# A hybrid decoder block on one Trainium2 core: the first norm's row factors applied to results, a transposed copy of the input, and rearranged sums and buffers around the feed-forward part

## The chip, the cores and the metric

The kernel runs on one core of one Trainium2 chip. The metric is the device time of one execution in microseconds (us); the predicted number is the median of runs of the changed kernel. One core has a matrix engine (PE, TensorE), a vector engine (DVE, VectorE), an activation engine (ACT, ScalarE), a general engine (POOL, GpSimd) and an engine that here only issues transfers (SP). Each has its own queue, worked off in order; transfers run on 16 DMA engines.

## The reference

```python
h = rms_norm(x, norm_mix_w)                 # x: 1024 rows x 1024
proj = h @ w_in                             # queries, K/V, gates, retention q/k/v/gate, merge gates
o_a = nsa_attention(...)                    # compressed, selected and window branches
y_a = o_a @ w_nsa_branch                    # 512 -> 1024
o_r = head_group_norm(retention(...)) * silu(g_ret)
y_b = o_r @ w_ret_branch                    # 1024 -> 1024
gate_a, gate_b = split(sigmoid(g_merge))
x = x + (gate_a * y_a + gate_b * y_b) @ w_mix_out
h = rms_norm(x, norm_ffn_w)
u = causal_dwconv(h @ w_ffn_up)             # 1024 -> 2 x 2816, width 3
x = x + (silu(u_gate) * u_val) @ w_ffn_down # 2816 -> 1024
return rms_norm(x, norm_final_w)
...
def rms_norm(x, w):
    return x * rsqrt(mean(x * x, -1) + EPS) * w
```

All values are float32. `rms_norm` is a row factor times x times a gain for each column, so a product of `h` with weights is the row factor times the product of (x times gain) with them.

## The kernel before

**Products.** A float32 value is held as two parts, a high one (rounded to fp32r by ACT) and a low one (the difference, from DVE or POOL): `split` (L174). Each product of 128 rows by 512 columns and 128 of depth is three matmuls, high by high, high by low, low by high (`mm3`, L278). Weights come by a 512 KB transfer into one of two raw slots (`wraw`), and are then split into five pairs of slots `wh`, `wl` (`Weights`, L181).

**Stages in the order of time.** (1) For each of eight row tiles x is loaded, squared and summed on ACT, brought to a row factor by small DVE steps (`normed`, L262), multiplied on DVE, transposed by eight PE transposes (`transposed_split`, L269) and split into `hh`, `hl`. (2) Projections of keys and values, block compression, queries. (3) Attention, by a planner that sets the order; the merge gates' raw projections (L784) fill PE between and go to DRAM as `gate_d`. (4) Retention. (5) The merges: first stage, eight steps (L1006 to L1018), each a gate loaded and passed through a sigmoid (`gated`, L976), 24 matmuls with `w_a` into one of two 1024-wide PSUM tiles (`ps2`), a DVE multiply that frees that tile (L1012), and eight transposes of `o_r` with their splits; second stage, eight steps of 48 matmuls with `w_b` (L1031 to L1042). (6) The output projection `w_mix` in two halves of columns (L1122, L1139), the second with the second norm and the transposes (`piece`, L1078). (7) The up projection for 22 column tiles f (`up`, L1235), and (8) the down projection in seven groups (`PRODUCTS`, L1408).

**Seven products in place of eight.** Up and down are each cut into 2 by 2 blocks and computed with seven products of sums of blocks. For down the sums of weight blocks (t1 to t4) are made ahead and put in DRAM: `t_sums` (L986), one for each j below 11: four loads of 256 KB, four DVE subtractions and four stores. For up the weights' sums are made just before use (`other_weights`, L1210), and those of activations in `sums` (L1154), after subtractions between row pieces in `piece`. The first product of each of five tiles (`LEAD`, L1191) runs before the sums are ready. Two lines of this make tiles wait for each other:

```python
m = mp.tile([P, S], F32, name=f"ma{j % KT}" if j < KT else "gb", bufs=1 if j < KT else 3)
...
(mp.tile([P, S], F32, name="tq", tag="gb", bufs=3) for _ in range(2))
```

The raw weight sums `tq` and the gates of the second stage share three slots `gb`; the first stage's gates have eight tiles `ma0` to `ma7` of their own. All transfers go through SP's queue in the order in which the scheduler puts them; one that waits for its slot holds up those behind it.

Of the kernel before, what the change touches and what calls it, by code (L numbers as in the profile page):

```python
# [14 lines left out]
OP = mybir.AluOpType  # L15
# [148 lines left out]
def hybrid_block(ctx: ExitStack, tc: tile.TileContext, a, c, out):  # L164
# [153 lines left out]

    with tc.tile_pool(name="n1", bufs=2, side="right") as n1:
        gain = n1.tile([P, D], F32, name="gain1", bufs=1)  # L320
        for t in range(NT):
            xt = big.tile([P, D], F32, name="big")
            n = 2 if t == 0 else 1
            for i in range(0, D, D // n):
                nc.sync.dma_start(xt[:, i:i + D // n], a["x"][0, t * P:(t + 1) * P, i:i + D // n])
            if t == 0:
                nc.sync.dma_start(gain, bcast_rows(a["norm_mix_w"][0], D))
                nc.sync.dma_start(ident, c["ident"])
            h = big.tile([P, D], F32, name="big")
            normed(n1, xt, gain, h, n)  # L330
            transposed_split(psA, h, hh, hl, t)
            if t < 2:
                kvw.more()
                kvw.more()
# [42 lines left out]
    def k_store(b, t, ps):  # L377

        ks = np_.tile([P, G, DH], F32, name="ks", bufs=2)
        nc.scalar.activation(ks, ps, AF.Copy)  # L380
# [12 lines left out]

    def v_store(b, t, ps):
        split(vhl[b][:, t, :, 0:DH], vhl[b][:, t, :, DH:], ps)
# [6 lines left out]
    def evac_kv(t, ps):  # L402
        nc.scalar.activation(kvc[:, t].rearrange("p a g d -> p (a g d)"), ps[:, 0:256], AF.Copy)
        k_store("s", t, g64(ps[:, 256:384]))
        v_store("s", t, g64(ps[:, 384:512]))
# [4 lines left out]
    def evac_kw(t, ps):  # L410
        k_store("w", t, g64(ps[:, 0:128]))
        v_store("w", t, g64(ps[:, 128:256]))
        nc.vector.tensor_copy(gates[:, t].rearrange("p h b -> p (h b)"), ps[:, 256:280])
# [90 lines left out]
    def evac_q(t, ps):  # L504
        nc.scalar.activation(qsb[:, t].rearrange("p h d -> p (h d)"), ps, AF.Copy, scale=DH ** -0.5)
        rope16(qsb[:, t], t, H, np_)
# [296 lines left out]
    nc.sync.dma_start(rope, c["rope128"])  # L803
    dmask = rp.tile([P, RH, P], F32, name="dmask")
# [26 lines left out]
    for p in range(2):  # L831
# [48 lines left out]
        def values(t, ps):  # L880
            v = big.tile([P, 2, 2, DV], F32R, name="v", tag="big")
            split(v[:, 0], v[:, 1], ps.rearrange("p (h e) -> p h e", h=2))
# [121 lines left out]
    for ch in range(2):  # L1004
        nx = Weights(w_a, 0, 4, [(512, 512)]) if ch == 0 else Weights(w_b, 0, KT, [(0, 512)])
        for i in range(4):  # L1006
# [7 lines left out]
            if len(t_left) > 5:  # L1014
                x, y = ([q[:, 0:512], q[:, 512:S]] for q in
                        (mp.tile([P, S], F32, name="tq", tag="gb", bufs=3) for _ in range(2)))
                t_sums(t_left.pop(0), x, y)
            transposed_split(ps1, o_r[ch * 4 + i], *orT, ch * 4 + i)  # L1018
        gw = nx
    with ort:  # L1020
# [8 lines left out]
        for ch in range(2):  # L1029
            nx = Weights(w_b, 0, KT, [(512, 512)]) if ch == 0 else Weights(w_mix, 0, KT, [(0, 512)])  # L1030
            for i in range(4):  # L1031
# [10 lines left out]
                ml.append(mlj)  # L1042
            gw = nx
# [34 lines left out]
    def piece(t, h):  # L1078
# [18 lines left out]
        side = nc.vector if t == NT - 1 else nc.gpsimd  # L1097
        nc.vector.tensor_tensor(b11, b12, b11, OP.subtract)
        side.tensor_tensor(b12, b22, b12, OP.subtract)
        nc.vector.tensor_tensor(b22, b22, b11, OP.subtract)  # L1100
        side.tensor_tensor(b21, b21, b22, OP.subtract)
# [65 lines left out]
    def raw_up(f, i):  # L1167
        r = wraw.tile([P, 2, 512], F32, name="wr")
        nc.sync.dma_start(r.rearrange("p a b -> p (a b)"), a["w_ffn_up"][f][:, i * 1024:(i + 1) * 1024])
        return r  # L1170

    def first_weights(f):

        g = raw_up(f, 0)
        p = parts2(g, nc.gpsimd)
        return {k: [x[:, i] for x in p] for i, k in enumerate(("a11", "a12"))}, g
# [12 lines left out]
    sums([4, 5])  # L1189
    uw, begun = {}, {}  # L1190
    for f in range(LEAD):  # L1191
        uw[f], _ = first_weights(f)
        begun[f] = start_up(uw[f])
# [9 lines left out]
    cpool = ups.enter_context(tc.tile_pool(name="cp", bufs=8, reuse_waits="tile"))  # L1203
# [6 lines left out]
    def other_weights(f, w, g=None):  # L1210
        v = raw_up(f, 1)
        g = g or raw_up(f, 0)
# [22 lines left out]
    def up(f, w, begun=None):  # L1235
        x, p1 = begun or start_up(w)
# [12 lines left out]
        if not begun:  # L1249
            prod(x, w["a12"], "21", False, True)  # L1250
# [12 lines left out]
    def weights(f):  # L1263
        if f in uw:
            return other_weights(f, uw.pop(f))
        return other_weights(f, *first_weights(f))

    nx = weights(0)
    for f in range(FT):
        w, nx = nx, weights(f + 1) if f + 1 < FT else None  # L1270
        up(f, w, begun.pop(f, None))
    tp.close()
    ups.close()


    STEPS = [(j, min(2, HT - j)) for j in range(0, HT, 2)]
    NS = len(STEPS)
# [5 lines left out]
    W = {"b11": (0, 0), "b21": (1, 0), "b22": (1, 1)}  # L1283
    A = {"a11": (0, 0), "a12": (1, 0), "a21": (0, 1), "a22": (1, 1)}
    kept = {}

    def fetch_a(k, i, dst):
# [3 lines left out]
        return dst  # L1291

# [33 lines left out]
    def prepared(sk, tk, i):  # L1326
        j, n = STEPS[i]
        t = wraw.tile([P, 2, 512], F32, name="wr")
        if tk in W:
            kh, nh = W[tk]  # L1330
            r0 = (kh * HT + j) * P
            src = w_dn[r0:r0 + n * P, nh * 512:nh * 512 + 512].rearrange("(k p) n -> p k n", p=P)
        else:
            src = t_d[int(tk[1]) - 1][j:j + n].rearrange("k p n -> p k n")
        nc.sync.dma_start(t[:, :n], src)
# [78 lines left out]
    ready = {}  # L1414
# [4 lines left out]
    for at, (i, j) in enumerate(units):  # L1419
# [3 lines left out]
        if i == 1:  # L1423
            held("a21", j)
# [40 lines left out]
_LAYOUT = {"w_ffn_up": _up_layout}  # L1465
# [22 lines left out]
```

## Time and profile before

| | |
|---|---|
| runs | 1814.02, 1811.32, 1814.24 us, median 1814.02 |
| the profiled execution | 1812.5 us, span 1810.7 us |
| PE busy | 1750.6 us (97%) |
| DVE, ACT, POOL busy | 1186.5, 804.2, 126.6 us |
| mean granted PE clock | 0.99 of full speed (2.4 GHz) |
| transfers | 178.88 MB |

The profile is of one execution. Its busy time of PE is time in which a matmul was in the engine, at whatever clock was granted; what PE did not do in the span is 60 us. Times in the rows below are from the span's start.

### The profile page before, as it was taken

The page shows a single profiled execution, that of the slowest core. Times are in us where ns is not written, and L with a number is a line of the kernel's source. Part 1 is how long each engine was busy: PE and PEld are TensorE (multiplying, and loading weights), DVE is VectorE, ACT ScalarE, POOL GpSimd, SP SyncE. Part 2 cuts the span into 40 slices and gives each one's busy share as a digit, 9 for nine tenths or more (in the row PEclk, how much of TensorE's full clock was granted, in tenths as well). Part 3 has the DMA queues.
Part 4 walks back from the last instruction along what each step waited for, and adds up shares of the span by engine and source line. Part 5 has one row for each costly group of instructions (what it writes and reads, how often), then busy time and mean ns, then how long its engine had stood idle before and what let it go on. Part 6 is the DMA issues. An engine that isn't in the chain of part 4 may idle for free.

```text
span 1810.7 us, 22500 instructions
## 1 busy us (share of the span) xinstructions
PE 1750.6 (97%) x8331; PEld 1434.6 (79%) x8331; DVE 1186.5 (66%) x2337; ACT 804.2 (44%) x1464; POOL 126.6 (7%) x78
## 2 busy tenths in 40 slices
PE   7999999999999999999989999789999999999998
PEld 6987888888788888888868877667888888878886
DVE  7445877777875554455644446767767777678666
ACT  6334666666662344136332215434444444343344
POOL 0000020110100000000000002301121211000000
PEclk9999999999999999999989999899999999999999
DMA  6121010110202111101682383322322322395353
GB/s 227 55 82 53 19 56 32 36 59 18 71 24 94 47 37 57 47 1 47 231 270 93 93 300 137 99 70 70 104 71 82 93 70 87 108 354 189 94 163 111
DMA packets 87418, 178.88 MB, mean 99 GB/s; under 512 B 8508, under 2 KB 18316, under 8 KB 87308
## 3 DMA queue, kind: packets, MB, share of 16 engines
q1 hardware_dynamic: 87308, 177.44, 30.2%
q8 instruction: 65, 1.06, 0.2%
q14 instruction: 45, 0.37, 0.1%
HBM read 137.57 MB, written 39.85 MB: 98 GB/s over the span
## 4 chain that ended last, share of the span: by engine, by line
PE 60%; DVE 5%; DMA 4%; ACT 2%; issue 2%; SPq 1%; POOL 1%; DVEq 0%; POOLq 0%; ACTq 0%
PE f L283 33%; PE mm L283 19%; PE fill L772 2%; DMA tq<-in_w_ffn_down 2%; PE po L826 1%; PE pv L718 1%; PE pt L706 1%; PE sc L610 1%; DMA wr<-in_w_ffn_up 1%; PE pst L826 1%; DMA wr<-in_w_mix_out 0%; ACT wh L209 0%; PE pss L871 0%; DVE c L1231 0%; DVE c L1232 0%
## 5 line engine op out<-in xcount | busy, mean ns | idle before, releaser
L283 PE MATMUL mm<-wh,hh 128*128 128x512 f32 (+1 forms) x576 | 224.0, 389 | 0.5 <-ACT hh L175 0.5
L283 PE MATMUL mm<-wh,hl 128*128 128x512 f32 (+1 forms) x576 | 219.8, 382 | 0.0
L283 PE MATMUL mm<-wl,hh 128*128 128x512 f32 (+1 forms) x576 | 219.8, 382 | 0.0
L209 ACT ACTIVATE wh<-wr 128x1024 fp32r<-128x1024 f32 (+1 forms) x72 | 74.6, 1037 | 167.0 <-PE mm L283 83.2
L713 DVE TENSOR_TENSOR pl<-pt,ph 128x512 fp32r<-128x512 f32 (+1 forms) x148 | 100.6, 686 | 41.8 <-ACT ph L710 41.2
L283 PEld LDWEIGHTS mm<-wh,hl 128*128 128x128 f32 x576 | 108.8, 189 | 20.6 <-DVE hl L176 0.3
L283 PEld LDWEIGHTS mm<-wh,hh 128*128 128x128 f32 x576 | 108.8, 189 | 20.2 <-ACT hh L175 0.9
L283 PE MATMUL f<-wh,sh 128*128 128x512 f32 x308 | 121.6, 395 | 3.3 <-ACT sh L175 3.3
L710 ACT ACTIVATE ph<-pt 128x512 fp32r<-128x512 f32 (+1 forms) x148 | 87.7, 594 | 82.8 <-PE pt L706 74.5
L283 PEld LDWEIGHTS mm<-wl,hh 128*128 128x128 f32 x576 | 108.9, 189 | 19.5 <-DVE wl L215 0.5
L283 PE MATMUL f<-wl,sh 128*128 128x512 f32 x308 | 121.5, 395 | 0.0
L283 PE MATMUL f<-wh,sl 128*128 128x512 f32 x308 | 120.7, 395 | 0.0
L283 PE MATMUL f<-bh,wh 128*128 128x512 f32 x264 | 105.0, 398 | 11.9 <-ACT c L1186 11.9
L176 POOL TENSOR_TENSOR wl<-wr,wh 128x1024 fp32r<-128x1024 f32 x22 | 53.6, 2438 | 898.3 <-ACT wh L175 883.4
L283 PE MATMUL f<-bht,wh 128*128 128x512 f32 x264 | 104.8, 397 | 8.3 <-ACT wh L175 8.3
L772 PE MATMUL fill<-hh,wh 128*128 128x512 f32 x256 | 104.5, 408 | 3.0 <-ACT sg L784 2.0
L283 PE MATMUL f<-bht,wl 128*128 128x512 f32 x264 | 105.0, 398 | 2.2 <-DVE wl L176 2.2
L628 ACT ACTIVATE big<-big,st 128x640 f32<-128x640 f32 (+7 forms) x128 | 93.4, 730 | 28.1 <-DVE st L624 27.3
L215 DVE TENSOR_TENSOR wl<-wr,wh 128x1024 fp32r<-128x1024 f32 (+1 forms) x60 | 71.5, 1193 | 51.2 <-ACT wh L209 50.2
L283 PE MATMUL f<-blt,wh 128*128 128x512 f32 x264 | 104.4, 395 | 0.0
L283 PE MATMUL f<-bl,wh 128*128 128x512 f32 x264 | 104.1, 394 | 0.0
L283 PE MATMUL f<-bh,wl 128*128 128x512 f32 x264 | 103.4, 393 | 0.0
(282 smaller groups left out, 4127.6 us busy)
## 6 DMA issues: line engine op xcount, KB each, us to landing
wr<-in_w_ffn_up SPq DMA_DIRECT2D x49, 512.0 KB, 4.7
wr<-in_w_in SPq DMA_DIRECT2D x40, 512.0 KB, 3.7
tq<-in_w_ffn_down SPq DMA_DIRECT2D x44, 256.0 KB, 4.7
t<-tq SPq DMA_DIRECT2D x44, 256.0 KB, 3.0
act<-c SPq DMA_DIRECT2D x22, 512.0 KB, 2.8
wr<-t SPq DMA_DIRECT2D x20, 512.0 KB, 3.5
a<-act SPq DMA_DIRECT2D x33, 256.0 KB, 6.0
gate<-sg SPq DMA_DIRECT2D x32, 256.0 KB, 2.0
```

Source lines behind the costliest of these rows:

```text
L176: (engine or nc.vector).tensor_tensor(lo, src, f32(hi), OP.subtract)
L209: nc.scalar.activation(hi[:, :, :self.n], self.raw[len(self.hi)], AF.Copy)
L215: self.engine.tensor_tensor(lo[:, :, :self.n], self.raw[j], f32(self.hi[j][:, :, :self.n]), OP.subtract)
L283: nc.tensor.matmul(ps, stat(sp, kt), mov(mp, kt), start=(first and n == 0), stop=(last and n == 3 * nk - 1), skip_group_check=more)
L610: nc.tensor.matmul(out[:, c0:c0 + n], q[:, h, :], mov, start=(q is box["h"]), stop=(q is box["l"]))
L628: nc.scalar.activation(probs[b][h], probs[b][h], AF.Exp, scale=-1.0, bias=stat["nm", b][:, h:h + 1], accum_out=stat["w", b][:, h:h + 1])
L706: nc.tensor.transpose(bx["pt"][:rows, h, :], probs[h][:, k * P:k * P + rows], ident)
L710: nc.scalar.activation(bx["h"][:rows], bx["pt"][:rows], AF.Copy)
L713: nc.vector.tensor_tensor(bx["l"][:rows], bx["pt"][:rows], f32(bx["h"][:rows]), OP.subtract)
L718: nc.tensor.matmul(acc["pv"], v, bx[part][:rows].rearrange("p h q -> p (h q)"), start=start, stop=stop)
L772: nc.tensor.matmul(fx["ps"], w.at(sp, kt, i * P, P), hT[mp][:, kt, half * 512:half * 512 + 512], start=(n == 0), stop=(n == 3 * KT - 1))
L826: nc.tensor.matmul(ps[:, h, :], stat[sp][:, h, :], mov[mp][:, h, :], start=(first and n == 0), stop=(last and n == 2))
```

## The change

**Row factors.** x is loaded twice: transposed (`x_t`, a second copy in DRAM that the host prepares) in pieces of 128 columns, that is rows of 512 bytes, and as before. The transposed tile times the gain (now one value for a partition) is split directly into `hh`, `hl`. The row factor `rs` is computed beside it and multiplied in where results leave PSUM: as the scale of ACT's copies, in `scaled_split`, in the two halves of retention's table `rope`, in the branch gates. For the merge gates, which lie transposed in DRAM, `rs` goes to DRAM and comes back broadcast (`rb`), and POOL multiplies each loaded gate by it before the sigmoid.

**Weight sums of down.** In the first merge stage every second step makes one (4, before the first 6), three are made in the second stage in `ma` tiles that are no longer needed, and four in the output projection at t = 0, 1, 2, 4 (before 5, at t = 1, 3, 5, 6, 7). The `gb` ring has two slots in place of three.

**Up and down.** All of `piece`'s subtractions are on DVE, `sums` stands behind the loop over the five first products; the second half of the weights, v, has its own two slots, the first half g is loaded a second time for every f (before: for f below 5) and its sums are made in place; the ring `c4` has 6 tiles in place of 8. Down's first pair of operands is fetched and split ahead of the last `up`.

```diff
+            xt = big.tile([P, KT, P], F32, name="big")
+            src = a["x_t"].rearrange("(k p) s -> p k s", p=P)[:, :, t * P:(t + 1) * P]
...
+                nc.sync.dma_start(xt[:, ks], src[:, ks])
+                if t == 0 and k == 0:
+                    kvw.fetch()
+                nc.vector.tensor_mul(xt[:, ks], xt[:, ks],
+                                     gain[:, ks, None].to_broadcast([P, KT // n, P]))
+                split(hh[:, ks, t * P:(t + 1) * P], hl[:, ks, t * P:(t + 1) * P], xt[:, ks])
...
-            normed(n1, xt, gain, h, n)
-            transposed_split(psA, h, hh, hl, t)
...
+            nc.sync.dma_start(x, a["x"][0, t * P:(t + 1) * P, :])
+            *_, v = mean_square(n1, [x], [x])
+            nc.vector.tensor_copy(rs[:, t:t + 1], rstd_of(n1, v))
...
+    def scaled_split(hi, lo, src, t):
+        r = rs[:, t:t + 1]
+        nc.scalar.activation(hi, src, AF.Copy, scale=r)
+        nc.vector.scalar_tensor_tensor(lo, src, r, f32(hi), op0=OP.mult, op1=OP.subtract)
...
+    for i in range(2):
+        nc.vector.tensor_mul(rope[:, i], rope[:, i], rs[:, :, None].to_broadcast([P, NT, DK // 2]))
...
-            nc.scalar.activation(sg, ps, AF.Silu)
+            nc.scalar.activation(sg, ps, AF.Silu, scale=rs[:, t:t + 1])
...
+    rb = mp.tile([P, S], F32, name="rb")
+    nc.sync.dma_start(rb, bcast_rows(rs_d, S))
...
-        m = mp.tile([P, S], F32, name=f"ma{j % KT}" if j < KT else "gb", bufs=1 if j < KT else 3)
+        m = mp.tile([P, S], F32, name=f"ma{j % KT}" if j < KT else "gb", bufs=1 if j < KT else 2)
         nc.sync.dma_start(m, gate_d[j])
+        nc.gpsimd.tensor_tensor(m, m, rb, OP.mult)
         nc.scalar.activation(m, m, AF.Sigmoid)
...
-            if len(t_left) > 5:
+            if (ch * 4 + i) % 2 == 0:
...
+                if j in (2, 4, 6):
+                    x, y = ([q[:, 0:512], q[:, 512:S]] for q in
+                            (mp.tile([P, S], F32, name="tq", tag=f"ma{j - k}") for k in (2, 1)))
+                    t_sums(t_left.pop(0), x, y)
...
-        if t in (1, 3, 5, 6, 7) and len(t_left):
+        if t in (0, 1, 2, 4):
...
-    sums([4, 5])
...
-            t = waiting[0][0]
             piece(*waiting.pop(0))
-            sums([t])
-        prod(begun[f][0], uw[f]["a12"], "21", False, True)
+        prod(begun[f][0], fw[f]["a12"], "21", False, True)
+    sums([4, 5, 6])
+    sums([7])
...
-    cpool = ups.enter_context(tc.tile_pool(name="cp", bufs=8, reuse_waits="tile"))
+    cpool = ups.enter_context(tc.tile_pool(name="cp", bufs=6, reuse_waits="tile"))
...
+        v = cpool.tile([P, 2, 512], F32, name="v", bufs=2)
+        nc.sync.dma_start(v.rearrange("p a b -> p (a b)"), a["w_ffn_up"][f][:, 1024:])
+        g = raw_up(f)
...
-        s2 = c4()
-        nc.vector.tensor_sub(s2[:, 0], g[:, 0], v[:, 0])
-        nc.vector.tensor_sub(s2[:, 1], g[:, 1], s[:, 1])
-        p = parts2(s2, nc.vector)
+        nc.vector.tensor_sub(g[:, 0], g[:, 0], v[:, 0])
+        nc.vector.tensor_sub(g[:, 1], g[:, 1], s[:, 1])
+        p = parts2(g, nc.vector)
...
+        if f == FT - 1:
+            s = fetch_a("a11", 0, wraw.tile([P, 2, 512], F32, name="wr"))
+            ready[0, 0] = [parts2(s, nc.vector), parts2(fetch_t("b11", 0), nc.vector)]
+        up(f, w)
```

How the order of instructions moves is shown at three places.

**SP's queue, start of the first merge stage.** `ma` are gates, `tq` the loads of a weight sum, `t` its stores, `rb` the broadcast row factors. Before:

```order
L978 DMA ma_8544<-gate_1643 128x1024
L989 DMA tq<-in_w_ffn_down 128x512
...
L978 DMA ma_8601<-gate_1644 128x1024
L997 DMA t_8523<-tq 128x512
L989 DMA tq<-in_w_ffn_down 128x512
L990 DMA tq<-in_w_ffn_down 128x512
L997 DMA t_8525<-tq 128x512
L997 DMA t_8524<-tq 128x512
L997 DMA t_8526<-tq 128x512
L978 DMA ma_8658<-gate_1645 128x1024
```

After:

```order
L1002 DMA rb<-rs_d 128x1024
L1006 DMA ma_8474<-gate_1569 128x1024
L1018 DMA tq<-in_w_ffn_down 128x512
...
L1006 DMA ma_8532<-gate_1570 128x1024
L1026 DMA t_8453<-tq 128x512
L1006 DMA ma_8576<-gate_1571 128x1024
L1026 DMA t_8455<-tq 128x512
L1026 DMA t_8454<-tq 128x512
L1026 DMA t_8456<-tq 128x512
L1006 DMA ma_8634<-gate_1572 128x1024
```

Before, all four stores and two of the next sum's loads stand ahead of the third gate; after, the third gate stands behind one store, and the next sum's loads behind the fourth gate.

**ACT's queue around the first evacuation of the five first products** (L1186 before, L1217 after, both `p1`; `bht` are high parts of `sums`, `h,ss` squares of the second norm, `rs_s` its square root, `wh` an up weight). Before:

```order
L256 ACTIVATE h,ss<-c_9866 128x512
L175 ACTIVATE bht_10398<-pc 128x4x128 x2
L256 ACTIVATE h,ss<-c_10324 128x512
L175 ACTIVATE bht_10400<-pc 128x4x128
L233 ACTIVATE rs_s<-rs_v 128x1
L175 ACTIVATE bht_10400<-pc 128x4x128
L175 ACTIVATE bht_10402<-pc 128x4x128 x2
L175 ACTIVATE bht_10404<-pc 128x4x128 x2
L1186 ACTIVATE c_10441<-f 128x512
```

After:

```order
L256 ACTIVATE h,ss<-c_9826 128x512
L175 ACTIVATE bht_10342<-pc 128x4x128
L175 ACTIVATE wh<-wr 128x1024
L256 ACTIVATE h,ss<-c_10268 128x512
L175 ACTIVATE bht_10342<-pc 128x4x128
L175 ACTIVATE bht_10344<-pc 128x4x128
L233 ACTIVATE rs_s<-rs_v 128x1
L1217 ACTIVATE c_10369<-f 128x512
```

Five `bht` fewer stand between the square root and this copy, three in place of eight ahead of it in all, and one weight's high part more.

**DVE's queue in the up stage** (a weight sum is L1214 to L1220 before, L1246 to L1251 after, with `wl`, its low part; L1240, L1244, L1248 before, L1271, L1275, L1279 after take products out of PSUM; L1259 and L1290 are the last multiply of the tile before). Before:

```order
L1215 TENSOR_TENSOR c_10802<-c_10802,wr 128x512
L1219 TENSOR_TENSOR c_10809<-wr 128x512
L1220 TENSOR_TENSOR c_10809<-wr,c_10802 128x512
L1259 TENSOR_TENSOR c_10787<-c_10787,c_10792 128x1024
L176 TENSOR_TENSOR wl<-c_10802,wh 128x1024
L176 TENSOR_TENSOR wl<-c_10809,wh 128x1024
L1240 TENSOR_TENSOR c_10833<-f,c_10502 128x512
```

After:

```order
L1247 TENSOR_TENSOR c_10744<-c_10744,wr 128x512
L1271 TENSOR_TENSOR c_10774<-f,c_10422 128x512
L1250 TENSOR_TENSOR wr<-wr,v 128x512
L1290 TENSOR_TENSOR c_10729<-c_10729,c_10734 128x1024
L176 TENSOR_TENSOR wl<-c_10744,wh 128x1024
L1251 TENSOR_TENSOR wr<-wr,c_10744 128x512
L1275 TENSOR_TENSOR c_10789<-f,c_10774 128x512
L1279 TENSOR_TENSOR c_10805<-f,c_10789 128x512
L176 TENSOR_TENSOR wl<-wr,wh 128x1024
```

Before, a whole weight sum with both low parts stands ahead of the next products' copies; after, copies stand between its steps.

## Rows read from the trace of the kernel before

**Rows 1.** Busy time by stretches: length, each engine's busy time, clock, DMA.

```profile
core 0: us, PE busy (x) PEld busy (x) DVE busy (x) ACT busy (x) POOL busy (x), PEclk, DMA share, GB/s
...
20.00:66.50 46.50, 46.50 (x236) 37.97 (x235) 27.56 (x94) 22.88 (x67) 1.48 (x4) 1.00 0.37 119
...
872.20:911.30 39.10, 39.10 (x194) 32.32 (x194) 25.58 (x33) 14.85 (x19) 0.00 (x0) 1.00 0.91 304
911.30:934.40 23.10, 15.30 (x57) 11.25 (x57) 15.61 (x21) 7.26 (x11) 0.00 (x0) 0.85 0.85 286
934.40:951.00 16.60, 16.57 (x51) 11.62 (x52) 3.87 (x5) 4.24 (x4) 0.00 (x0) 0.69 0.68 236
951.00:1027.60 76.60, 76.60 (x340) 63.42 (x339) 33.56 (x28) 20.89 (x20) 0.00 (x0) 1.00 0.24 75
...
1193.00:1238.00 45.00, 34.51 (x131) 25.88 (x131) 33.81 (x40) 16.43 (x19) 2.59 (x2) 0.93 0.32 105
1238.00:1584.80 346.80, 346.80 (x1502) 281.89 (x1502) 252.35 (x287) 148.09 (x161) 62.07 (x34) 1.00 0.27 85
```

**Rows 2.** Waits of PE over the span: total, times, longest.

```profile
PE f L283 <- ACT c L1186: 11.9, 4, 7.0
PE tp L275 <- DVE big L267: 8.7, 1, 8.7
PE f L283 <- ACT wh L175: 8.3, 4, 3.6
PE mm L283 <- DVE ma L1012: 4.8, 3, 2.6
PE f L283 <- ACT sh L175: 3.3, 1, 3.3
PE tp L275 <- DVE orT L176: 3.0, 2, 2.5
```

**Rows 3.** Timeline of PE and ACT in the first 22 us.

```profile
8.65 1.97 PE L275 MATMUL tp<-ident,big 128*128 128x128 f32 x8 [8.65 <-DVE big L267]
11.15 0.80 PE L283 MATMUL mm<-wh,hh 128*128 128x512 f32 x1 [0.54 <-ACT hh L175]
...
17.26 1.03 PE L275 MATMUL tp<-ident,big 128*128 128x128 f32 x8
18.19 0.50 PE L283 MATMUL mm<-wl,hh 128*128 128x512 f32 x1
...
15.81 1.06 ACT L209 ACTIVATE wh<-wr 128x1024 fp32r<-128x1024 f32 x1 [1.31 <-DMA wr<-in_w_in]
```

**Rows 4.** Chain that ended last, in the merges: start, us, what.

```profile
875.66 4.89 DMA tq<-in_w_ffn_down
...
917.53 6.05 DMA ma<-gate
923.60 1.07 ACT ma L979
```

**Rows 5.** Timeline of DVE and POOL around 1123 and 1134 us.

```profile
1123.66 2.19 DVE L239 SCALAR_TENSOR_TENSOR rs_t<-rs_y,rs_v 128x1 f32<-128x1 f32 x1
...
1134.32 0.21 DVE L239 SCALAR_TENSOR_TENSOR rs_t<-rs_y,rs_v 128x1 f32<-128x1 f32 x1
...
1123.42 2.42 POOL L176 TENSOR_TENSOR wl<-wr,wh 128x1024 fp32r<-128x1024 f32 x1 [1.02 <-ACT wh L175]
```

**Rows 6.** Groups of DVE's instructions from 872 to 951 us.

```profile
L993 DVE TENSOR_TENSOR tq<-tq 128x512 f32<-128x512 f32 x6 | 4.1, 686 | 2.3 <-DMA tq<-in_w_ffn_down 2.3
```

**Rows 7.** Timeline of ACT around the merge to the up stage.

```profile
1077.57 1.06 ACT L209 ACTIVATE wh<-wr 128x1024 fp32r<-128x1024 f32 x1 [9.70 <-DMA wr<-in_w_mix_out]
...
1133.07 2.69 ACT L175 ACTIVATE bht<-pc 128x512 fp32r<-128x512 f32 x5
1135.67 0.57 ACT L1186 ACTIVATE c<-f 128x512 f32<-128x512 f32 x1
```

More of the change, by code (lines that the diff above doesn't have):

```diff
@@ L379, in k_store @@
         ks = np_.tile([P, G, DH], F32, name="ks", bufs=2)
-        nc.scalar.activation(ks, ps, AF.Copy)
+        nc.scalar.activation(ks, ps, AF.Copy, scale=rs[:, t:t + 1])
         rope16(ks, t, G, np_)
@@ L394, in v_store @@
     def v_store(b, t, ps):
-        split(vhl[b][:, t, :, 0:DH], vhl[b][:, t, :, DH:], ps)
+        scaled_split(vhl[b][:, t, :, 0:DH], vhl[b][:, t, :, DH:], ps, t)
     kvc = np_.tile([P, NT, 2, G, DH], F32, name="kvc")
@@ L504, in evac_q @@
     def evac_q(t, ps):
-        nc.scalar.activation(qsb[:, t].rearrange("p h d -> p (h d)"), ps, AF.Copy, scale=DH ** -0.5)
+        nc.scalar.activation(qsb[:, t].rearrange("p h d -> p (h d)"), ps, AF.Copy,
+                             scale=rs_q[:, t:t + 1])
         rope16(qsb[:, t], t, H, np_)
@@ L1013, in hybrid_block @@
             ma.append(m)
-            if len(t_left) > 5:
+            if (ch * 4 + i) % 2 == 0:
                 x, y = ([q[:, 0:512], q[:, 512:S]] for q in
-                        (mp.tile([P, S], F32, name="tq", tag="gb", bufs=3) for _ in range(2)))
+                        (mp.tile([P, S], F32, name="tq", tag="gb", bufs=2) for _ in range(2)))
                 t_sums(t_left.pop(0), x, y)
@@ L1248, in up @@
         nc.vector.tensor_add(cv[:, 1], z, u3)
-        if not begun:
-            prod(x, w["a12"], "21", False, True)
+        if f >= LEAD:
+            prod(x, fw[f]["a12"], "21", False, True)
         nc.scalar.activation(cg[:, 0], x, AF.Copy)
@@ L1261, in up, with fetch_a, fetch_t @@
         nc.sync.dma_start(act_d[f], yg)
[L1263 to L1268, printed above, removed]
-    for f in range(FT):
-        w, nx = nx, weights(f + 1) if f + 1 < FT else None
-        up(f, w, begun.pop(f, None))
+    STEPS = [(j, min(2, HT - j)) for j in range(0, HT, 2)]
+    NS = len(STEPS)
+    A = {"a11": (0, 0), "a12": (1, 0), "a21": (0, 1), "a22": (1, 1)}
+    W = {"b11": (0, 0), "b21": (1, 0), "b22": (1, 1)}
+    def fetch_a(k, i, dst):
+        (kh, sh), (j, n) = A[k], STEPS[i]
+        for x in range(n):
+            nc.sync.dma_start(dst[:, x], act_d[kh * HT + j + x][:, sh])
+        return dst
+    def fetch_t(k, i):
+        j, n = STEPS[i]
+        t = wraw.tile([P, 2, 512], F32, name="wr")
+        if k in W:
+            kh, nh = W[k]
+            r0 = (kh * HT + j) * P
+            src = w_dn[r0:r0 + n * P, nh * 512:nh * 512 + 512].rearrange("(k p) n -> p k n", p=P)
+        else:
+            src = t_d[int(k[1]) - 1][j:j + n].rearrange("k p n -> p k n")
+        nc.sync.dma_start(t[:, :n], src)
+        return t
+    ready = {}
+    nx = other_weights(0)
+    for f in range(FT):
+        w, nx = nx, None
+        if f + 1 < FT:
+            if f + 1 >= LEAD:
+                fw[f + 1] = first_weights(f + 1)
+            nx = other_weights(f + 1)
+        if f == FT - 1:
+            s = fetch_a("a11", 0, wraw.tile([P, 2, 512], F32, name="wr"))
+            ready[0, 0] = [parts2(s, nc.vector), parts2(fetch_t("b11", 0), nc.vector)]
+        up(f, w)
     tp.close()
     ups.close()
-    STEPS = [(j, min(2, HT - j)) for j in range(0, HT, 2)]
-    NS = len(STEPS)
     keep = ctx.enter_context(tc.tile_pool(name="keep", bufs=1, side="right", reuse_waits="tile"))
@@ L1282, in hybrid_block @@
     kp2 = ctx.enter_context(tc.tile_pool(name="keep2", bufs=1, reuse_waits="tile"))
-    W = {"b11": (0, 0), "b21": (1, 0), "b22": (1, 1)}
-    A = {"a11": (0, 0), "a12": (1, 0), "a21": (0, 1), "a22": (1, 1)}
     kept = {}
-    def fetch_a(k, i, dst):
-        (kh, sh), (j, n) = A[k], STEPS[i]
-        for x in range(n):
-            nc.sync.dma_start(dst[:, x], act_d[kh * HT + j + x][:, sh])
-        return dst
     def held(k, i):
@@ L1326, in prepared @@
     def prepared(sk, tk, i):
[L1327 to L1335, printed above, removed]
+        n = STEPS[i][1]
+        t = fetch_t(tk, i)
         s = S_OF[sk](i)
@@ L1423, in hybrid_block @@
         if i == 1:
+            held("a11", j)
             held("a21", j)
@@ L1481 @@
     a = {k: given(k, _LAYOUT.get(k, lambda v: v)(v)) for k, v in inputs.items()}
+    a["x_t"] = given("x_t", inputs["x"][0].T)
     c = {k: given("c_" + k, v) for k, v in _constants().items()}
```

63 lines of the change are left out of this document (33 added, 30 removed).

## Prediction

> **What bounds the kernel now.** I read the busy time by stretches first. PE is the bound nearly everywhere: from 1238 to 1584.8 us it is busy for all of 346.8 us while DVE works 252.35, ACT 148.09 and POOL 62.07 [rows 1]. There only fewer or faster matmuls help, and attention and retention read the same way. What can be gained lies in the few stretches in which PE has less to do than the stretch is long, and in those at a low clock: 911.3 to 934.4 us (15.30 busy of 23.10, clock 0.85), 934.4 to 951 (fully busy, but clock 0.69, so between the levels 2.4 and 1.2 GHz), 1193 to 1238 (34.51 of 45.00) [rows 1]. Next, PE's waits say who ends each pause: 8.7 us at the start for the first norm's multiply, 11.9 for the copy of the first up products, 8.3 for split up weights, 4.8 and 3.0 in the merges for the gate multiply L1012 and for a transposes' split, 3.3 for down's first operand [rows 2]. Then the timelines and the chain, for what stands behind each: at the start PE transposes from 8.65 us and multiplies from 11.15 [rows 3]. In the merges the chain runs through transfers, one weight-sum load of 4.89 us after the other, up to a gate that lands after 6.05 us, its sigmoid at 923.60 and only then the multiply [rows 4]: the gate is late because SP's queue puts it behind stores that wait for DVE.
>
> **The start.** Removed are 64 transposes. Their eight before the first product take 1.97 us, and a later eight hold the stream from 17.26 to 18.19, 0.93 us [rows 3]. The first product no longer waits for squares, row factor, gain over 1024 columns (512 KB, now 4 KB) and transposes, only for the transposed tile, a multiply and a split. I expect it near 7.5 us in place of 11.15, but the second half of the weights still comes through two raw slots: at 15.81 ACT had been waiting 1.31 us for a transfer of weights [rows 3]. So of the 3.6 us I count 2.4, and of the seven later groups of transposes six (the first falls into that wait): 6 times 0.93 is 5.6. Together **-8**. Added is a second load of x, 4 MB, half of it in 512-byte rows whose price no row shows. A tile of x is 24 matmuls, which at 0.227 us apart (the trace of the second stage has 340 in 76.6 us [rows 1]) is 5.4 us. The stage of merges moves 304 GB/s at a share of 0.91 [rows 1]; at that rate both loads of a tile, 1 MB, take 3.4 us, and if 512-byte rows ran at half of it, 5.2 us, just under 5.4. From 20 to 66.5 us the engines are at a share of 0.37 [rows 1], so the room is there. Bounds: -10 (all 3.6 and seven groups) and 0 (the transposed rows supply worse than half, and the gain goes).
>
> **The scales on results** change forms, not numbers of instructions: a copy on ACT with a scale, one DVE operation in place of another. I cost them at nothing; their cover is DVE, busy 0.73 of the full stretch above and less in attention, and PE beside it. Were it gone, some 100 operations at 0.1 us more would be 10 us of DVE, still under that cover.
>
> **The merges.** By count of matmuls: 194 of the first stage take 39.10 us, 0.2015 each, so the next 57 should take 11.5 and take 23.1; 340 of the second take 76.60, 0.2253 each, so the 51 from 934.4 should take 11.5 and take 16.6 [rows 1]. That is 11.6 and 5.1 lost, 16.7 in all, of which 7.8 are PE's waits [rows 2] and the rest half clock after them. What removes it: in SP's new order the third gate stands behind one store in place of four and two loads, the fourth ahead of the next sum's loads, and the sums fall from six to four in a stage that is full of transfers (0.91). A gate then lands a step or more ahead. What is added is a POOL multiply of 128x1024 per gate; the nearest row is POOL's subtraction of that size, 2.42 us [rows 5]. A step of the first stage is 24 matmuls and 8 transposes, 32 at 0.2015, 6.45 us, and eight multiplies are 19.4 us in 51.6: it fits if the gate comes 2.42 + 1.07 us (sigmoid [rows 4]) ahead of the step's end. I count **-16**, bounds -16.7 and +3.
>
> Here the trace warns: a DVE operation of one column takes 0.21 us alone and 2.19 beside POOL's subtraction, ending with it at about 1125.8 [rows 5]. DVE works 25.58 and 15.61 us in the first stage [rows 1]; two sums fewer are eight subtractions of 0.686 [rows 6], so 35.7 of 51.6 remain, 15.9 spare. If each of eight multiplies held DVE for all of its 2.42 us, that would be 19.4, 3.5 more than is spare, hence a bound of about +3 for the stage; at half of it, 9.7, it is hidden.
>
> The Trainium skill, page "SBUF — State Buffer", section "SBUF: two separate sides", speaks against this part of the change: VectorE and GpSimd share a port pair as an exclusive lock, and a VectorE operation with two SBUF inputs fully blocks against a GpSimd operation that reads SBUF. The 2.19 us agrees with it. By the rule only the weight sums, the low parts of weights and the adds of the second stage would be held, not the gate multiply, which reads PSUM; the stage's sum would be worse by 0 to 3.5 us. The rival below prices the full block.
>
> **The second merge stage** takes in three weight sums: PE is busy throughout, DVE 33.56 of 76.60 [rows 1], so 12 subtractions of 0.686, 8.2 us, and eight POOL multiplies are hidden. With `gb` at two slots its first gates come after the last stores of the first stage; that is part of the +3.
>
> **The output projection's first half** has the sums at t = 0, 1, 2, 4. The last weights for the second half were split at 1077.57 after 9.70 us of waiting for their transfer [rows 7]; PE stood 2.9 us around it. Without late sums ahead in the queue: **-3**, bounds -3 and 0.
>
> **The first up products.** The copy L1186 begins at 1135.67, behind five `bht` that end there [rows 7], while PE has waited 7.0 us of its 11.9 [rows 2]. In the new order those five stand behind it, 2.69 us, but a weight's high part of 1.06 us (as at 1077.57 [rows 7]) comes ahead, in time ACT mostly idles. I count **-2**, bounds -3 and +1 (all of `piece`'s subtractions on DVE: four more of 0.69).
>
> **Up.** The stalls from 1193 to 1238 are 10.5 us [rows 1]. Copies now stand between the steps of the weight sums on DVE, and g is fetched again. The low parts still come behind the conv and the silu of the tile before; I count **0**, bounds -12 and +5. From f = 5 on there are 512 KB more in each tile of some 18 us (346.8 over 19 tiles), 28 GB/s on 85; c4's six slots in place of eight I cost at nothing, the cover being PE's fully busy 346.8 us.
>
> **Down's start.** PE waits 3.3 us for the first operand [rows 2]. It is now fetched and split ahead of the last `up`: **-2.7**, bounds -3.3 and 0.
>
> **Sum.** -8 - 16 - 3 - 2 - 2.7 = -31.7 from the profiled 1812.5 us: 1780.8. The runs' median, 1814.02, is 1.5 above the profiled execution; with it 1782.3, rounded up to **1783** for small losses.
>
> **The rivals.**
> - *POOL holds the merges.* Each gate needs load, POOL, sigmoid; if DVE and POOL block each other fully, ps2's two tiles come free late, PE pauses again and falls to the low clock. The merges then give 6 in place of 16: 1793. For it, 2.19 against 0.21 us [rows 5]; against it, half a step of spare time on both engines.
> - *The start gains nothing*, since 512-byte rows or SP's queue are slow: 1791. For it, the 1.31 us of waiting for weights [rows 3]; against it, the share of 0.37 [rows 1].
> - *The up stage's stalls go too*, since copies no longer stand behind a whole sum: 10.5 less, 1772. For it, 8.3 us of waiting for weight parts [rows 2]; against it, the order of low parts behind the conv.
> - *Slower than before.* The second fetch of g takes one of two raw slots, and its sums are made in place, so the slot comes free only after the last split; if that delays each tile of up, in which PE now never waits, the price is 22 times the delay. It decides from 31.7 / 22 = 1.44 us a tile: at 2 us the time is 1783 + 44 = 1827. For it, DVE at 0.73 and three transfers of 512 KB a tile on one queue; against it, 18 us to fit them in.
> - *It does nothing*: the start, the merges and down's start all stay as they are, 1814.
>
> **How the numbers follow.** Chances: forecast 0.53 (its own range 1777 to 1788), POOL holds the merges 0.14, no gain at the start 0.10, up's stalls go 0.12, slower 0.06, nothing 0.05. The predicted time is the forecast's, 1783. The range reaches from 1771, with up's stalls gone, to 1800, which takes in the first two rivals with a few us of the unknown bounds; beyond lie the last two and some of each side. A change of 0.2%, 3.6 us, is about what a measurement of this kernel tells from none. Faster 0.88, within it 0.05, slower 0.07.
>
> **What would show it.** Start: PE's first instruction a product near 7.5 us and the key projection's end near 58 in place of 66.5 us [rows 1]. Merges: no wait for the gate multiply over 1 us, clock 1.00 from 911 to 951 us of the old scale, gates loaded a step ahead, POOL's multiplies about 2.4 us each. Output projection: no wait for `in_w_mix_out`. Down: PE's pause before its first product under 1 us. The forecast is wrong if PE waits in the merges for L1041 (the multiply's new line) or in up's later tiles for weights, or if the matmuls of the first 60 us have gaps.

## The result, and the profile after

The changed kernel takes 1791.49 us (median of four runs, 1788.04 to 1798.61) against 1814.13 (four runs, 1811.32 to 1814.28): a ratio of 0.9884, interval 0.9849 to 0.9919. It is faster by 22.6 us, of 31 forecast, and inside the stated range. The profiled execution is the slowest of the four, 1798.61 us with a span of 1796.7; a second profile of the same kernel (the first experiment) has 1791.57 and 1789.6, so both are used.

Stages, in us, cut at PE's timeline: PE's first instruction of the compression (L462 of the changed kernel), the last product ahead of `oaT`, the last one with `orT`, the last with `ml`, the last with `bh`, the last of all. The 7.1 to 7.7 us of the span behind the last product are left out. The other columns are experiments told below; "best" is the last of them.

| stage | before | changed | changed, again | no multiply | old norm | best |
|---|---|---|---|---|---|---|
| start and key projection | 69.65 | 66.44 | 64.76 | 64.57 | 69.78 | 62.12 |
| compression to retention | 801.86 | 803.19 | 801.94 | 803.57 | 803.08 | 803.07 |
| both merge stages | 156.23 | 150.95 | 147.61 | 140.17 | 142.26 | 142.31 |
| output projection | 97.91 | 100.54 | 99.27 | 95.39 | 95.50 | 96.23 |
| up, with the five first products | 459.59 | 451.30 | 451.80 | 450.53 | 453.21 | 451.33 |
| down | 218.25 | 216.57 | 216.56 | 216.57 | 216.56 | 216.55 |

Busy time by stretches of the changed kernel, columns as in [rows 1]:

```profile
core 0: us, PE busy (x) PEld busy (x) DVE busy (x) ACT busy (x) POOL busy (x), PEclk, DMA share, GB/s
6.00:26.00 20.00, 16.20 (x44) 11.18 (x45) 13.73 (x26) 12.02 (x20) 0.00 (x0) 0.83 1.03 324
...
869.60:926.90 57.30, 53.09 (x251) 43.08 (x250) 41.14 (x40) 21.29 (x28) 19.84 (x8) 0.97 0.77 258
926.90:932.50 5.60, 2.58 (x17) 1.72 (x14) 5.53 (x8) 2.35 (x4) 0.00 (x0) 1.00 0.61 199
...
1069.60:1121.10 51.50, 47.90 (x223) 39.09 (x224) 32.51 (x71) 26.57 (x62) 5.21 (x2) 0.97 0.41 141
...
1176.00:1222.00 46.00, 37.65 (x140) 28.36 (x138) 34.52 (x41) 16.63 (x17) 2.57 (x2) 0.87 0.23 78
1222.00:1572.40 350.40, 349.46 (x1511) 285.44 (x1512) 254.96 (x291) 149.21 (x164) 63.41 (x34) 0.99 0.34 110
```

PE is still short of work at the same places, but by less: the first merge stage has 53.09 busy in 57.30, and 2.58 of the 5.60 us behind it. DVE is busy in the first merge stage for 41.14 us, not the 35.7 that two sums fewer should have left. PE's waits, to be held against [rows 2]:

```profile
PE mm L283 <- ACT wh L209: 8.1, 3, 7.0
PE mm L283 <- DVE ma L1041: 7.1, 5, 2.9
PE f L283 <- ACT wh L175: 5.6, 3, 2.4
PE f L283 <- ACT c L1217: 4.6, 4, 2.3
PE f L283 <- DVE wl L176: 3.6, 4, 1.2
PE f L283 <- ACT wh L209: 2.9, 1, 2.9
...
PE mm L283 <- DVE vs L354: 1.6, 1, 1.6
```

Of the first row 7.0 us are the time to the first product. The waits for the first up products (11.9) and for down's first operand (3.3) have gone to 4.6 (6.3 in the second profile) and away. The wait for the gate multiply has not gone: before it was 4.8 us, here it is 7.1, and in the second profile of the same kernel 4.0:

```profile
PE mm L283 <- DVE ma L1041: 4.0, 3, 3.0
```

This is so although the gates land earlier (the sixth at 912.10 us; before at 923.58 [rows 4]). Why is seen in the timelines of the first merge stage, POOL's, DVE's, SP's queue and PE's:

```profile
912.17 2.86 POOL L1007 TENSOR_TENSOR ma<-ma,rb 128x1024 f32<-128x1024 f32 x1 [4.15 <-DMA ma<-gate]
915.23 2.58 POOL L1007 TENSOR_TENSOR ma<-ma,rb 128x1024 f32<-128x1024 f32 x1 [0.20 <-DMA ma<-gate]
...
912.79 2.78 DVE L1023 TENSOR_TENSOR tq<-tq 128x512 f32<-128x512 f32 x1
915.61 2.74 DVE L1024 TENSOR_TENSOR tq<-tq 128x512 f32<-128x512 f32 x1
918.28 1.21 DVE L1041 TENSOR_TENSOR ma<-mm,ma 128x1024 f32<-128x1024 f32 x1
...
915.61 3.10 SPq L1026 DMA_DIRECT2D t<-tq  x3
...
919.55 0.74 PE L283 MATMUL mm<-oaT,wh 128*128 128x512 f32 x2 [2.48 <-DVE ma L1041]
```

Two of a weight sum's subtractions take 2.78 and 2.74 us in place of 0.686 [rows 6]; each begins while a POOL multiply runs and ends about 0.55 us after that multiply's end (915.03 and 917.81). The gate multiply stands behind them on DVE, its sigmoid done (ACT begins it at 915.06), and PE waits 2.48 us for the PSUM tile. SP's queue stands too: its three stores take 3.10 us, until the last subtraction is done, and the next gate and the next sum's loads are queued behind them. The longest of the five waits, 2.94 us ahead of the product at 932.53, goes along with that: the next sum's loads land late, and three of its subtractions, at their own 0.69 us by then, stand on DVE ahead of the last gate multiply.

### The profile page after: what moved, and what is told of

It reads as the page before. It is cut to its first block, busy times and chain, and to the rows that moved or that the text cites. A ratio compares the mean times of both kernels' runs of the same rounds, so it can differ in the third digit from the quotient of the medians.

```text
span 1796.7 us, 22466 instructions
## 1 busy us (share of the span) xinstructions
PE 1744.6 (97%) x8267; PEld 1430.9 (80%) x8267; DVE 1205.6 (67%) x2347; ACT 809.5 (45%) x1455; POOL 162.2 (9%) x88
## 5 line engine op out<-in xcount | busy, mean ns | idle before, releaser
L209 ACT ACTIVATE wh<-wr 128x1024 fp32r<-128x1024 f32 (+1 forms) x72 | 74.5, 1036 | 135.1 <-PE mm L283 65.8
L175 ACT ACTIVATE wh<-wr 128x1024 fp32r<-128x1024 f32 (+1 forms) x87 | 88.2, 1020 | 97.7 <-DVE wr L1251 45.8
```

Source lines behind the costliest of these rows:

```text
L175: nc.scalar.activation(hi, src, AF.Copy)
L209: nc.scalar.activation(hi[:, :, :self.n], self.raw[len(self.hi)], AF.Copy)
```

## Experiments

Each is an edit of the changed kernel, timed beside the kernel before. The base is the first. The runs were made in four batches, in which the kernel before has medians of 1813.37 (the first four), 1810.68 (the next four), 1810.29 (the two after) and 1812.91 us (the last); so runs of different batches are compared by their ratios, and a difference of their medians is rough by some 3 us.

| run | median us | ratio to before, interval |
|---|---|---|
| changed, again | 1793.97 | 0.9908, 0.9890 to 0.9925 |
| no multiply | 1781.36 | 0.9831, 0.9813 to 0.9850 |
| multiply on DVE | 1788.88 | 0.9868, 0.9850 to 0.9886 |
| long rows | 1792.19 | 0.9895, 0.9876 to 0.9914 |
| two sums later | 1794.72 | 0.9907, 0.9890 to 0.9923 |
| fourth sum earlier | 1792.39 | 0.9900, 0.9882 to 0.9917 |
| no early down | 1799.95 | 0.9934, 0.9917 to 0.9950 |
| first products undone | 1800.61 | 0.9941, 0.9924 to 0.9958 |
| old norm | 1786.38 | 0.9859, 0.9842 to 0.9875 |
| multiply on DVE, long rows | 1783.02 | 0.9845, 0.9820 to 0.9869 |
| best: that, weights first | 1781.31 | 0.9834, 0.9820 to 0.9849 |

**The changed kernel again.** No edit.

> The changed kernel once more, as the base of the other runs and because its four runs spread over 10.6 us (1788.04 to 1798.61) while the profiled one was the slowest of them. If the spread lies in one stage (a transfer that lands late now and then), this profile shows PE's waits of the start (10 us in all before), of the merges (7.1 us for the gate multiply L1041) or of the output projection (2.9 us) changed by several us; if it is small amounts everywhere, the waits are the same to about 1 us. I expect a median of 1788 to 1793.

The two profiles differ by 7 us, most of it in the start (64.76 against 66.44) and in the merges (147.61 against 150.95), the rest in the compression to retention and the output projection, not in one late transfer; six runs lie between 1791.57 and 1798.94. Over all profiles below that leave a place unchanged, the start takes 64.57 to 67.79 us and the merges 147.61 to 150.95. Differences below 3 us between these runs are therefore not read.

**No multiply.**

```diff
-    rb = mp.tile([P, S], F32, name="rb")
-    nc.sync.dma_start(rb, bcast_rows(rs_d, S))
...
-        nc.gpsimd.tensor_tensor(m, m, rb, OP.mult)
```

> Leaves out the multiplication of the merge gates by the row factors and its broadcast load. Theory (POOL's multiplies hold DVE's weight-sum subtractions: 2.9 us instead of 0.69 in the trace of the changed kernel, and with them the gate multiply behind them): all subtractions take about 0.69 us, PE's 7.1 us of waits for L1041 go, with some 3 us of half clock after them: 8 to 11 us less than the changed kernel. Rival (the gates are late because of SP's order and the transfers): the waits for L1041 stay, and the time falls by less than 3 us.

12.6 us less: 7.4 in the merges, about as expected, and 3.9 in the output projection, which was not. DVE's groups in the first merge stage, of the changed kernel and then of this run (busy, mean ns; lines of this run are 4 lower):

```profile
L1041 DVE TENSOR_TENSOR ma<-mm,ma 128x1024 f32<-128x1024 f32 x7 | 8.5, 1214 | 4.4 <-ACT ma L1008 4.4
L1024 DVE TENSOR_TENSOR tq<-tq 128x512 f32<-128x512 f32 x3 | 6.3, 2112 | 0.1
L1023 DVE TENSOR_TENSOR tq<-tq 128x512 f32<-128x512 f32 x3 | 5.5, 1835 | 0.1
L1021 DVE TENSOR_TENSOR tq<-tq 128x512 f32<-128x512 f32 x4 | 5.1, 1266 | 7.3 <-DMA tq<-in_w_ffn_down 7.3
```

```profile
L1020 DVE TENSOR_TENSOR tq<-tq 128x512 f32<-128x512 f32 x4 | 2.8, 690 | 0.1
L1017 DVE TENSOR_TENSOR tq<-tq 128x512 f32<-128x512 f32 x4 | 2.8, 690 | 5.6 <-DMA tq<-in_w_ffn_down 5.6
L1019 DVE TENSOR_TENSOR tq<-tq 128x512 f32<-128x512 f32 x4 | 2.7, 687 | 0.1
```

Without POOL's multiply every subtraction takes 0.69 us, and PE waits in the merges once, for 0.9 us:

```profile
PE mm L283 <- DVE ma L1037: 0.9, 1, 0.9
```

The first theory holds; the rival, SP's order, would have left the waits. The merges' 140.17 us are 16.1 less than before: the rest of the change in this stage, sums and slots together, brings what the prediction's term said.

**The multiply on DVE.** `nc.gpsimd.tensor_tensor(m, m, rb, OP.mult)` becomes `nc.vector.tensor_tensor(m, m, rb, OP.mult)`.

> The multiply of the gates by the row factors on DVE in place of POOL. If what hurts is POOL holding DVE, the cost becomes 16 times 1.22 us of DVE, of which the first stage has room for eight, and most of what the run without a multiply gains is kept: 5 to 10 us less than the changed kernel. If what hurts is one more step between a gate's landing and its sigmoid, or DVE's total work, it is the same or up to 5 us slower.

5.1 us less than the base, the intervals just apart. The same number of multiplies, half as long and with the subtractions at their own length:

```profile
L1007 DVE TENSOR_TENSOR ma<-ma,rb 128x1024 f32<-128x1024 f32 x8 | 9.7, 1219 | 1.0 <-DMA ma<-gate 1.0
...
L1023 DVE TENSOR_TENSOR tq<-tq 128x512 f32<-128x512 f32 x4 | 2.7, 686 | 0.1
```

The merges take 141.45 us in this profile, 1.3 more than without a multiply. So in the merges it is where the multiply runs that hurt, not one step more ahead of the sigmoid. The other 7.5 us that the run without a multiply gains are not kept here: the output projection takes 98.67 us in place of 95.39, and the start, whose code is the same, 66.20 in place of 64.57.

**Long rows.**

```diff
-            src = a["x_t"].rearrange("(k p) s -> p k s", p=P)[:, :, t * P:(t + 1) * P]
+            src = a["x_t"][t].rearrange("p (k s) -> p k s", s=P)
...
-    a["x_t"] = given("x_t", inputs["x"][0].T)
+    a["x_t"] = given("x_t", inputs["x"][0].reshape(NT, P, KT, P).transpose(0, 3, 2, 1).reshape(NT, P, D))
```

> The transposed copy of x laid out so that each tile's row of a partition is 4 KB long, in place of eight rows of 512 bytes; same bytes. Theory (the start is bound by transfers, share 0.99 from 9.6 to 24 us at some 340 GB/s, and short rows are part of it): rates near the 380 to 410 GB/s of the kernel before, the last weights split 1 to 2 us earlier, the key projection ends 2 to 4 us earlier, 2 to 4 us less in all. Rival (the two raw weight slots bind): less than 1 us.

By stretches, the base and then this run:

```profile
13.00:26.00 13.00, 10.97 (x39) 8.05 (x40) 10.13 (x22) 9.34 (x16) 0.00 (x0) 0.87 1.09 341
```

```profile
13.00:26.00 13.00, 11.20 (x46) 8.48 (x46) 11.58 (x23) 9.91 (x21) 0.00 (x0) 1.00 1.01 402
```

The rate rises from 341 to 402 GB/s at a full share of the engines, and the start stage falls from 64.76 to 63.30, below all eight profiles with short rows. The time, 1.8 us less, is not told from none.

**Two sums later.** `(ch * 4 + i) % 2` becomes `% 4`, the second stage makes sums at j = 2 to 6 in the tiles `ma{j // 2 * 2 - k}`.

> The changed kernel with two of the first merge stage's four weight sums moved into the second stage (five there); the gate multiplies stay on POOL. Theory of the lock (only DVE operations with two SBUF inputs are held by POOL, in the first stage above all the weight sums): half of the held subtractions leave the first stage, so PE's waits for L1041 there fall from 4 to 7 us to about 2 and the first stage ends 0 to 3 us earlier, while more subtractions of the second stage are held; DVE has room there, so 2 to 6 us less in all than the changed kernel (about 1787 to 1790). Rival (POOL's multiply holds DVE whatever it does, or the added step itself is too long): same waits, same time within 2 us.

The merges fall to 142.05 us, but the output projection rises to 103.48, and the time is that of the base; the 2 to 6 us expected do not come. The theory's place is right, its sum wrong: the sums of the output projection begin 12.3 us after the last merge product in place of 7.5, and PE waits there 2.0 us for the merges' last split and 1.7 for the last weights.

**Fourth sum earlier.** The second merge stage makes one more, at j = 7, and the output projection makes its sums at t = 0, 1, 2.

> The changed kernel with the fourth weight sum of the output projection (at t = 4) made in the second merge stage instead. Theory (the last pair of output weights is issued late because the split that frees its raw slot stands on DVE behind that weight sum, whose load is awaited): PE's 1.6 to 2.9 us of waiting for L209 there and the half clock after it go, 3 to 5 us less. Rival (the slot is freed late by PE's own use of the split weights): the wait stays, the time is the same within 2 us.

PE's wait for the last weights falls to 0.86 us (1.6 in the base), but the two splits that free raw slots begin 38.4 and 41.2 us after the last merge product and the last weights are still issued at 42.9 (43.1 in the base). Merges and output projection together stay: 248.7 against 246.9 us. The expected 3 to 5 us do not come; which wait holds that last transfer is not settled by it.

**No early down.** Without the three lines at `f == FT - 1`.

> The changed kernel without the early fetch and split of down's first operands. By the prediction 2.7 us are lost again: PE waits 3.3 us for the first operand, 2 to 4 us slower than the changed kernel. Rival (the transfer is hidden otherwise, or the early fetch costs as much elsewhere): within 1 us.

```profile
PE f L283 <- ACT sh L175: 3.1, 1, 3.1
```

6.0 us more than the base by medians, about 4.7 by the ratios (0.9934 against 0.9908), of which the profile shows 3.96 in the down stage (220.52); the wait is back as the prediction said, and the rest lies below the spread.

**First products undone.** Sums at the old places, two subtractions on POOL:

```diff
-        nc.vector.tensor_tensor(b12, b22, b12, OP.subtract)
+        side = nc.vector if t == NT - 1 else nc.gpsimd
+        side.tensor_tensor(b12, b22, b12, OP.subtract)
...
+    sums([4, 5])
...
+            sums([t])
...
-    sums([4, 5, 6])
-    sums([7])
```

> The changed kernel with the sums of activations spread over the loop of the first products again and two of the subtractions between row pieces on POOL. By the prediction's term 2 us are lost; by the trace of the changed kernel, in which PE's waits for the first copies fell from 11.9 to between 4.6 and 6.3 us and PE runs parts of later products meanwhile, 5 to 8 us are lost. If the up stage's gain of 8 us comes from the interleaved weight sums instead, less than 2.

```profile
PE f L283 <- ACT c L1218: 8.9, 4, 5.6
```

6.6 us more by medians, about 6 by the ratios; the up stage takes 458.06 us, 6.3 to 6.8 more than in the two profiles of the changed kernel. So most of its gain comes from here, of the sums' places and the subtractions' engine together, which were not undone apart.

**Old norm.** All of the norm's part taken back: transposes on PE, no `x_t`, no scales on results, no multiply of the gates; the rest of the change stays.

```diff
-                nc.vector.tensor_mul(xt[:, ks], xt[:, ks],
...
+            normed(n1, xt, gain, h, n)
+            transposed_split(psA, h, hh, hl, t)
...
-        nc.gpsimd.tensor_tensor(m, m, rb, OP.mult)
```

> The changed kernel with the first norm and the scales on results as in the kernel before (transposes on PE, no transposed input, no multiply of the gates), all other parts of the change kept. If the norm part is worth the 8 us at the start and POOL's multiplies cost nothing, this is 8 us slower than the changed kernel, about 1800. By the runs so far the start gives only 2 to 6 us and the multiplies cost 12.6: then this is 6 to 10 us faster than the changed kernel, about 1783 to 1787, with the first merge stage near 50.5 us and the key projection ending as in the kernel before.

Faster than the changed kernel: 0.9859 against 0.9908, the intervals apart. The start is 69.78 us, as before; merges and output projection together take 237.8 us in place of 246.9. The norm's part, as it was made, costs more than it brings.

**The multiply on DVE and long rows.** Both edits from above.

> The changed kernel with the gate multiply on DVE and the transposed copy in 4 KB rows, the two edits that were faster or not slower alone. If they add: 5 us from the multiply and 1 to 2 from the rows, 1786 to 1788. If the start's gain is lost again behind it (attention starts earlier but ends the same), as the multiply alone, 1789.

1783.02 us, below the 1786 to 1788 expected: by the ratios 11 us less than the base, where the two edits alone had given 7 and 2. That is at least their sum; that it is more is not shown, as its four runs lie between 1778.58 and 1788.45. Start stage 63.67, merges 140.21.

**Weights first.** In addition:

```diff
-                for _ in range(3):
-                    kvw.more()
+                kvw.more()
+                for _ in range(2):
+                    kvw.fetch(big.tile([P, 2, 512], F32, name="big"))
+                    kvw.high()
+                    kvw.low()
```

> The run with the multiply on DVE and long rows, and in addition the third and fourth pairs of key weights loaded into two tiles of the ring `big` right behind the second, ahead of the first natural tile of x, in place of waiting for one of two raw slots. If the start lost what I expected because those weights come late (split at 12.1 and 15.2 us with long rows, PE stopping four times and staying at the low clock until about 20 us), they are split near 10 and 12 us, the first tile's products end 3 to 5 us earlier and so does the key projection: 2 to 4 us less in all than that run, about 1780. If the stage is bound by the transfers of x further on, or by the row factors that the copies wait for, the key projection ends within 1 us of that run.

```profile
9.48 1.06 ACT L209 ACTIVATE wh<-big 128x1024 fp32r<-128x1024 f32 x1 [0.29 <-DMA big<-in_w_in]
10.88 1.06 ACT L209 ACTIVATE wh<-big 128x1024 fp32r<-128x1024 f32 x1 [0.34 <-DMA big<-in_w_in]
```

The last two pairs are split 2.6 and 4.3 us earlier than with long rows alone (12.12 and 15.22), the start stage takes 62.12 us, 1.6 less than that run (3 to 5 were expected) and 7.5 less than before, close to the 8 of the prediction. The median, 1781.31, is not told from the run without this edit, but it is clear of the changed kernel (0.9834, up to 0.9849, against 0.9908, from 0.9890): this version beats both kernels. From the run with the old norm it is not clearly apart (0.9859, from 0.9842), so that the norm's part pays even in this form is not shown.

## Why the prediction was right within its range and where its steps failed

**The likeliest case did not come as told.** 1791.49 lies between two rivals, in which the start gains nothing (1791) and in which POOL holds the merges (1793); the mechanism is the second's, with part of the first's, and the sign of being wrong that the prediction named, PE's waits for L1041, is there. That the time is still within 8.5 us of the forecast is in part luck: the merges, the start and the output projection together gave 15 to 21 us less than their terms, and the first up products and up 6 us more than theirs, for a reason that the prediction did not have. The failed step of the merges is "at half of it, 9.7, it is hidden": DVE's total time was weighed against the stage, but the queue is in order. A held subtraction does not cost its own stretch only; the gate multiply that frees a PSUM tile stands behind it, and the store that SP's queue waits for. The row of 2.19 against 0.21 us [rows 5] was there, and so was the rule. The Trainium skill, page "SBUF — State Buffer", section "SBUF: two separate sides", says that a VectorE operation with two SBUF inputs and a GpSimd operation that reads SBUF exclude each other; the traces agree to the operand: three of the four subtractions from SBUF go from 0.69 us to means of 1266, 1835 and 2112 ns, the gate multiply with its PSUM input stays at 1214. In the second profile both run beside one POOL multiply:

```profile
879.65 2.38 POOL L1007 TENSOR_TENSOR ma<-ma,rb 128x1024 f32<-128x1024 f32 x1 [1.30 <-DMA ma<-gate]
...
879.54 1.22 DVE L1041 TENSOR_TENSOR ma<-mm,ma 128x1024 f32<-128x1024 f32 x1
880.68 1.90 DVE L1023 TENSOR_TENSOR tq<-tq 128x512 f32<-128x512 f32 x1
```

The first is not held, the second ends 0.55 us after POOL.

**The merges: -16, came as -5.3 and -8.6.** Of the term, the rearranged sums and slots bring -16.1 (no multiply) or -14.0 (old norm), and the multiply on POOL takes back 7 to 11.

**The start: -8, came as -3.2 and -4.9.** The first product begins at 6.99 us (7.5 expected), and no transposes stand in the stream. But the first tile's weights come late:

```profile
12.88 1.06 ACT L209 ACTIVATE wh<-wr 128x1024 fp32r<-128x1024 f32 x1 [1.31 <-DMA wr<-in_w_in]
16.49 1.06 ACT L209 ACTIVATE wh<-wr 128x1024 fp32r<-128x1024 f32 x1 [2.56 <-DMA wr<-in_w_in]
```

PE, begun earlier, stops four times for parts of weights, 0.2 to 0.9 us each, and runs from 6 to 26 us at a mean granted clock of 0.83, partly at 1.2 GHz. The clock goes along with part of the start's spread: from 13 to 26 us it is 0.74 in the changed kernel's first profile, with a start of 66.44 us, 0.87 in its second, with 64.76, and 1.00 without the multiply, with 64.57; but 1.00 stands beside 66.20 with the multiply on DVE. The step "the room is there" took the mean share from 20 to 66.5 us for the first 20; there the engines are full (share 1.03 at 324 GB/s from 6 to 26 us), and they nearly were in the kernel before:

```profile
13.00:26.00 13.00, 13.00 (x57) 10.34 (x57) 11.46 (x30) 9.51 (x21) 0.00 (x0) 1.00 0.87 293
```

The row quoted for 0.227 us a matmul gives 0.2253; the 5.4 us of a tile stay. A new wait of 1.6 us came beside this, for a tile's copies out of PSUM (L354), which the prediction did not have; what holds them was not tried. Weights first and long rows bring the start to -7.5.

**The output projection: -3, came as +2.6 and +1.4.** The wait for the last weights stayed, 2.9 us here and 1.6 in the second profile; before it was

```profile
PE f L283 <- ACT wh L209: 2.2, 1, 2.2
```

The term took it that fewer late sums clear the queue. In the two runs without any multiply of the gates the splits that free raw slots begin 37.4 to 37.5 us after the last merge product and the stage takes 95.4 to 95.5; in the changed kernel 41 to 43 and 99.3 to 100.5. That the sums there begin later (7.5 to 9.3 us after that product against 6.4 to 6.5) goes along with it, but is not the whole cause: the run with the fourth sum moved stayed at the same time, and other runs have late splits and a short stage (40.9 us and 95.79 with the multiply on DVE and long rows, 41.9 and 96.54 with the first products undone). In the last of these the final weights are issued as late as in the base, 43.4 us against 43.1, but their split begins 4.9 us after the issue in place of 6.4. What lengthens that transfer was not tried; why the term failed stays open.

**The first up products and up: -2 and 0, came as -8.3 and -7.8 together.** The order was read rightly, and the size was off. The term counted the durations of five `bht`, but in the kernel before ACT's queue stood ahead of them:

```profile
1130.34 0.63 ACT L175 ACTIVATE bht<-pc 128x512 fp32r<-128x512 f32 x1 [4.25 <-DVE pc L1100]
```

That `bht` waited 4.25 us for the row pieces' subtractions on DVE and POOL. In the changed kernel the copy begins at 1126.35 us, 5.2 after the output projection's last product, in place of 10.0:

```profile
1126.35 0.58 ACT L1217 ACTIVATE c<-f 128x512 f32<-128x512 f32 x1
```

In the run with the first products undone it begins 8.6 us after that product, and the up stage loses 6.3 to 6.8 us; the remaining 1.5 lie with what else changed there, the weight sums and their buffers among it, which were not tried apart. Up's stalls stayed (37.65 busy of 46.00, with 34.51 of 45.00 before [rows 1]): the term of 0 is right to 2 us.

**Down: -2.7, came as -1.7**, and 4 when taken back. **Scales on results: 0**, came as +1.3 and +0.1 from the compression to retention.

The rival that ends slower than before has no sign: PE is busy for 349.46 of the 350.40 us of up's later tiles.

## What to carry to other kernels

Work given to POOL is not free because POOL is idle: if DVE works on SBUF at the same time, price each collision at up to POOL's whole operation, and then look at what stands behind the held operation in DVE's in-order queue and in the queues that wait for it. A wait that ends at the head of a queue, not the sum of the instructions in it, is what a reordering removes; read the idle time ahead of the first of them. And a saving at the front of a kernel is worth only what the transfers there can supply: take the share of the same microseconds, not of the stage.

## What the runs showed of the hardware that was not expected

From 13 to 26 us, where the tiles of x come in by turns with the transposed ones, 341 to 348 GB/s were moved at a full share of the 16 engines in the eight profiles in which the transposed tiles have rows of 512 bytes, and 402 and 404 in the two in which they have 4 KB rows and nothing else changes at the start. The Trainium skill, page "DMA: Bandwidth & Descriptors", section "Specifications", gives 512 bytes as enough for line rate; the measurement here differs and decides. And POOL's own multiply, 2.37 to 2.42 us when alone, took 2.86 and 2.58 when it began beside one of DVE's subtractions: the hold works both ways.
